# A hybrid attention and conv-FFN layer in float32: weight pieces of 1024 columns in place of 2048

## The chip, the core and the metric

The kernel runs on one core of a Trainium2 chip. The metric is the time of one execution on the device in microseconds (us), lower being better; a version's time is the median of several executions. PE is TensorE, DVE VectorE, ACT ScalarE, POOL GpSimd and SP SyncE, which issues most DMAs here.

## What is computed

One layer on 256 tokens of width 2048, in float32. A projection of x feeds three groups of dilated attention (8 heads of 128), a gated linear attention (4 heads) and two gates; their outputs are projected, gated, summed and projected again; a residual sum and layer norm follow, then a feed-forward net with a short convolution along the tokens, and a second residual sum and layer norm. Cut to the products with weights:

```
def _mixer(x, ...):
    parts = jnp.split(x @ w_in, cuts, axis=-1)      # q, k, v of 3 groups; gq gk gv gr g_low m_a m_b
    ...
    ya = ... @ w_proj_a
    yb = (o * jax.nn.silu(gr)) @ w_proj_b
    y = jax.nn.sigmoid(m_a) * ya + jax.nn.sigmoid(m_b) * yb
    return y @ w_out

def _conv_ffn(x, w_gate, w_up, conv_w, conv_b, w_down):
    g = x @ w_gate
    gc = conv_b + sum(conv_w[i] * shifted(g, i) for i in range(CONV_W))
    return (jax.nn.silu(gc) * (x @ w_up)) @ w_down

def reference(x, ...):
    x = _layernorm(ALPHA * x + _mixer(x, ...))
    return _layernorm(ALPHA * x + _conv_ffn(x, ...))
```

## The kernel before

**Products of split numbers.** Each float32 operand is split into a part that the matmul takes exactly (hi, ACT's copy in L136) and the rest (lo = value − hi, DVE's subtraction in L137). A product is hi·hi + hi·lo + lo·hi, so PE uses each piece of weights as hi and as lo.

**Pieces.** All weights arrive as a stream of pieces of 128 partitions × 2048 columns (1 MB), laid out on the host by `_stream` in the order of their use. `load` issues a piece's DMA on SP into a buffer: for the first layer's first part the tag raw (2 buffers), later the tag quarter (6 buffers; `home` says which). `two_parts` takes the tile for hi (tag whi, 3 buffers) and for lo (wlo, 2) and calls `split`. A buffer is free when its last reader is done, and a DMA or a split into it waits for that. So a load runs ahead of PE by as many buffers as there are.

**Three forms of product.** `b16` makes 128 columns of the output from one piece: 16 hi matmuls of 512 columns (L228), then 16 lo matmuls of 256 (L230). Its result is summed by `b_sum` (ACT pa in L252, DVE in L253), which frees the PSUM bank. `a_chunk` makes 256 × 512 outputs from two or four pieces (nf/4 pieces in the FFN's down projection), with hi, lo, hi matmuls for each 128 rows of weights (L260 to L262), and calls `pump` behind each piece, which writes the next side job (gate parts, transposes, residual sums) into the program at that place. `seven` makes a block product with seven products instead of eight; it sums pieces into each other first, on DVE (`add`, L339) or, for two of the sums, by an adding DMA on POOL's queue (`add_by_dma`, L342). In its `part`, the eight hi matmuls of a piece come ahead of its four lo ones (L326).

**Order.** Program text order isn't the order on the engines: a scheduler places each engine's instructions by modelled times and by the buffers in the pools, so that other pieces change what stands next to what. Within an engine the order is then fixed, and an instruction that waits holds all behind it.

**The stages**, by the profile's time: 0 to about 850 us the projections of x, with `gkq`, `qk` and the `seven` blocks side by side with attention; 850 to 1125 the projections ya (`yp`), `pb` and `wo`, with `gated_out` and its transposes (L808, fed by sg of L837 to L839) as a side job; at 1125 the residual sum r (L903), the statistics (L904, L888) and the first layer norm (L914, transposes L921); from 1150 the FFN. The FFN's first tiles come as three at once (`b16_three`); then each step f sums the gate (gbuf, L253), convolves (gr, L962 to L964), takes its silu (sg, L966), sums the up product (yb, L253), multiplies (yb, L974) and splits into h (L136, L137). While the FFN begins, `gain` scales the residual r by rows of layer norm parameters (L937, L938), which POOL fetches by DMA as tiles called row. The FFN runs in four parts, each followed by its down projection (`wd`). From 1873 us the last sums and the second layer norm run alone.

Of the kernel before, what the change touches and what calls it, by code (L numbers as in the profile page):

```python
# [35 lines left out]
FSPLIT = (16, 16, 8, 4)  # L36

# [20 lines left out]
def hybrid_layer(ctx: ExitStack, tc: tile.TileContext, wp, xt, wgl, gw, par, relb, onehot, rows, xk, out):  # L58
# [80 lines left out]
    home = ["raw", 2]  # L139

    def raw_tile(i, tag=None, bufs=None):
        tag, bufs = (tag, bufs) if tag else home
        return wpool.tile([P, 2048], F32, tag=tag, name=f"{tag}_{i}", bufs=bufs)
# [168 lines left out]
    def seven(name, xs, comb, i, store, by_dma=True):  # L312
# [41 lines left out]
        def p5():  # L354
            st["B12"] = [get(2), get(3)]
# [5 lines left out]
        def p6():  # L361
            st["B22"] = [get(4), get(5)]
# [26 lines left out]
        def p2():  # L389
            st["B21"] = [get(6), get(7)]  # L390
# [126 lines left out]
    def gkq(which, h):  # L517
        st = {}

        def f(j, before=(None,)):  # L520
            def g():
                ps = b16("gqk", xop, AT["gkq", which] + 2 * h + j, before)
# [8 lines left out]
    def head(h):  # L531
# [3 lines left out]
        def f(g, which):  # L535
            def t():
                ps = b16("qk", xop, AT["qk", h] + 2 * g + which)
# [187 lines left out]
    def gkq_tiles():  # L725
        for which in range(2):
            for h in range(GH):
                f = gkq(which, h)
                yield f(0, [pair_of_x(j) for j in range(4)] if not which and not h else (None,))
# [52 lines left out]
    for n in range(2):  # L782
        pss = a_chunk("m", xop, 16, AT["mb"] + 4 * n, 3)
# [5 lines left out]
    home[:] = "quarter", 6  # L789
# [73 lines left out]
    for n in range(4):  # L863
        g = [gate(1, n, t) for t in range(2)]
        pss = a_chunk("pb", by_pairs(OB), 16, AT["pb"] + 4 * n)
# [30 lines left out]
    for n in range(4):  # L896
# [3 lines left out]
        pss = a_chunk("wo", by_pairs(YT), 16, AT["wo"] + 4 * n)  # L900
# [45 lines left out]
    for part, nf in enumerate(FSPLIT):  # L946
# [5 lines left out]
        for f in range(f0, f0 + nf):  # L952
            if f == 0:
                first = AT["fgu"]
                three = dict(zip("gun", b16_three(("fg", "fu", "fg"), x1op, (first, first + 1, first + 2))))
            at = AT["fgu"] + 2 * f
# [10 lines left out]
            if f == 1:  # L967
                with tc.issue_after(held.ins):
                    ps = b16("fu", x1op, at + 1)
            else:  # L970
                ps = three["u"] if f == 0 else b16("fu", x1op, at + 1)
# [12 lines left out]
        for n in range(0, 4, 2):  # L984
            at = [AT["wd", part] + (n + i) * nf // 4 for i in range(2)]
# [36 lines left out]
def _stream():  # L1022
# [121 lines left out]
```

## Time and profile before

| | us |
|---|---|
| median of three executions | 1892.54 (1891.72 to 1896.99) |
| profiled execution | 1894.48 |
| its span on the core | 1892.8 |

| instructions in the profiled execution | count | mean |
|---|---|---|
| lo splits of whole pieces from quarter, DVE L137 | 312 | 2289 ns |
| hi splits of whole pieces from quarter, ACT L136 | 312 | 1917 ns |
| lo and hi splits of whole pieces from raw | 71 and 71 | 2288 and 1914 ns |
| sums of pieces, DVE L339 | 44 | 2284 ns |
| loads of 1 MB into quarter and into raw | 252 and 71 | 4.9 and 6.8 us to landing |
| adding DMAs, POOL L342, 1 MB | 36 | 12.4 us to landing |

The page of a profile gives each engine's busy time; a view by stretch gives the same for parts of the span, with the granted TensorE clock (PEclk, 1.00 is full speed) and what the 16 DMA engines moved. A view of waits says which engine waited for whom. In a timeline's row stand the start, the duration (of x instructions together), the engine, the line, the tiles (output <- inputs, with shapes), and in brackets the idle time ahead of it and what ended it.

### The profile page before, as it was taken

The page shows a single profiled execution, that of the slowest core. Times are in us where ns is not written, and L with a number is a line of the kernel's source. Part 1 is how long each engine was busy: PE and PEld are TensorE (multiplying, and loading weights), DVE is VectorE, ACT ScalarE, POOL GpSimd, SP SyncE. Part 2 cuts the span into 40 slices and gives each one's busy share as a digit, 9 for nine tenths or more (in the row PEclk, how much of TensorE's full clock was granted, in tenths as well). Part 3 has the DMA queues.
Part 4 walks back from the last instruction along what each step waited for, and adds up shares of the span by engine and source line. Part 5 has one row for each costly group of instructions (what it writes and reads, how often), then busy time and mean ns, then how long its engine had stood idle before and what let it go on. Part 6 is the DMA issues. An engine that isn't in the chain of part 4 may idle for free. (4 is left out here: it accounts for less than half of the span.)

```text
span 1892.8 us, 23057 instructions
## 1 busy us (share of the span) xinstructions
PE 1837.2 (97%) x9270; PEld 1548.0 (82%) x9270; DVE 1310.8 (69%) x1186; ACT 970.1 (51%) x963; POOL 121.9 (6%) x205
## 2 busy tenths in 40 slices
PE   7989999999999999999899998999999999999996
PEld 6778887888888888787788877888888888888885
DVE  6879978888797888764755557666546665456557
ACT  5457555555656565544643344454335554345442
POOL 0001000100101000001300001000000000000001
PEclk9999999999999999999999998999999999999998
DMA  8468986978979779794965546555555555565551
GB/s 304 157 251 275 318 307 207 326 234 263 329 230 327 231 274 331 214 325 163 333 224 195 202 160 217 179 195 183 200 189 189 189 190 193 187 243 182 196 178 45
DMA packets 80134, 432.21 MB, mean 228 GB/s; under 512 B 9857, under 2 KB 20124, under 8 KB 34076
## 3 DMA queue, kind: packets, MB, share of 16 engines
q1 hardware_dynamic: 50252, 345.06, 49.4%
q0 software_dynamic: 16240, 73.52, 15.5%
q10 hardware_dynamic: 13536, 12.16, 2.1%
q8 instruction: 72, 1.18, 0.2%
q14 instruction: 34, 0.28, 0.0%
HBM read 372.97 MB, written 21.14 MB: 208 GB/s over the span
## 5 line engine op out<-in xcount | busy, mean ns | idle before, releaser
L137 DVE TENSOR_TENSOR wlo<-quarter,whi 128x2048 fp32r<-128x2048 f32 x312 | 713.4, 2289 | 358.8 <-ACT whi L136 82.1
L136 ACT ACTIVATE whi<-quarter 128x2048 fp32r<-128x2048 f32 x312 | 597.4, 1917 | 479.1 <-PE wd_t L262 106.4
L137 DVE TENSOR_TENSOR wlo<-raw,whi 128x2048 fp32r<-128x2048 f32 (+1 forms) x75 | 165.2, 2203 | 47.3 <-ACT whi L136 23.7
L136 ACT ACTIVATE whi<-raw 128x2048 fp32r<-128x2048 f32 (+1 forms) x75 | 138.4, 1845 | 110.5 <-PE qk L228 43.2
L228 PE MATMUL qk<-x,whi 128*128 128x512 f32 x768 | 193.1, 399 | 1.5 <-ACT whi L136 1.5
L228 PE MATMUL fu<-x,whi 128*128 128x512 f32 x688 | 165.9, 394 | 5.5 <-DVE yb L253 5.5
L228 PEld LDWEIGHTS qk<-x,whi 128*128 128x128 f32 x768 | 142.0, 188 | 32.6 <-ACT whi L136 2.2
L228 PE MATMUL fg<-x,whi 128*128 128x512 f32 x672 | 160.2, 390 | 0.0
L228 PEld LDWEIGHTS fu<-x,whi 128*128 128x128 f32 x688 | 127.7, 190 | 30.6 <-issue 5.7
L228 PEld LDWEIGHTS fg<-x,whi 128*128 128x128 f32 x672 | 123.7, 188 | 24.0
L260 PE MATMUL wd_t<-whi,h 128*128 128x512 f32 x352 | 137.0, 389 | 0.0
L261 PE MATMUL wd_t<-wlo,h 128*128 128x512 f32 x352 | 137.0, 389 | 0.0
L262 PE MATMUL wd_t<-whi,h 128*128 128x512 f32 x352 | 136.9, 389 | 0.0
L230 PEld LDWEIGHTS qk<-x,wlo 128*128 128x128 f32 x768 | 98.4, 191 | 4.0 <-DVE wlo L137 0.3
L339 DVE TENSOR_TENSOR quarter<-quarter,quarter 128x2048 f32<-128x2048 f32 x44 | 100.3, 2284 | 0.4
L230 PE MATMUL qk<-x,wlo 128*128 128x256 f32 x768 | 99.7, 283 | 0.0
L230 PEld LDWEIGHTS fu<-x,wlo 128*128 128x128 f32 x688 | 88.2, 191 | 3.4
L230 PE MATMUL fu<-x,wlo 128*128 128x256 f32 x688 | 89.2, 283 | 0.0
L230 PEld LDWEIGHTS fg<-x,wlo 128*128 128x128 f32 x672 | 86.2, 191 | 3.3
L230 PE MATMUL fg<-x,wlo 128*128 128x256 f32 x672 | 87.2, 283 | 0.0
L260 PEld LDWEIGHTS wd_t<-whi,h 128*128 128x128 f32 x352 | 66.1, 188 | 13.7
L261 PEld LDWEIGHTS wd_t<-wlo,h 128*128 128x128 f32 x352 | 66.1, 188 | 13.6
(316 smaller groups left out, 2680.3 us busy)
## 6 DMA issues: line engine op xcount, KB each, us to landing
quarter<-in_wp SPq DMA_DIRECT2D x252, 1024.0 KB, 4.9
raw<-in_wp SPq DMA_DIRECT2D x71, 1024.0 KB, 6.8
quarter<-quarter POOLq DMA_DIRECT2D x36, 1024.0 KB, 12.4
row<-in_rows POOLq DMA_DIRECT2D x16, 256.0 KB, 4.6
sp<-c POOLq DMA_DIRECT2D x14, 256.0 KB, 10.9
bias<-bvd ACTq DMA_DIRECT2D x32, 96.0 KB, 4.6
v<-vs ACTq DMA_DIRECT2D x24, 128.0 KB, 2.9
m<-sp POOLq DMA_DIRECT2D x12, 256.0 KB, 4.9
```

The lines of the kernel that those rows point to most:

```text
L136: nc.scalar.activation(hi, src, AF.Copy)
L137: nc.vector.tensor_tensor(lo, src, hi.bitcast(F32), op=ALU.subtract)
L228: nc.tensor.matmul(ps, parts(kc)[0], opnd(kc), start=(kc == 0), stop=False)
L230: nc.tensor.matmul(ps[:, S:], parts(kc)[1], opnd(kc)[:, :S], start=False, stop=(kc == nk - 1))
L260: nc.tensor.matmul(ps, xh, hi, start=first, stop=False)
L261: nc.tensor.matmul(ps, xh, lo, start=False, stop=False)
L262: nc.tensor.matmul(ps, xl, hi, start=False, stop=last)
L339: tt(a, a, b, op=ALU.add)
```

## The change

A piece has 1024 columns instead of 2048 (512 KB), and each tag has twice as many buffers of half the size: raw 4, quarter 12, whi 6, wlo 4. The bytes are the same. The stream is cut in halves in the same order of use. `b16` takes two pieces, of eight blocks of 128 each; `a_chunk` takes one for each two blocks of 128 rows instead of four, and still calls `pump` where it did, behind every second piece. In `seven` the order hi, hi, lo is kept within a piece, so that there are four hi matmuls and then two lo ones. So 323 loads by SP become 646, 383 splits of whole pieces on ACT and as many on DVE become 766 each (the first piece, which was already cut in four slices of 512, stays in four), 44 sums on DVE become 88, and 36 adding DMAs become 72. PE has the same matmuls.

```
 FSPLIT = (16, 16, 8, 4)
+PC = 1024
...
-    home = ["raw", 2]
+    home = ["raw", 4]
...
         tag, bufs = (tag, bufs) if tag else home
-        return wpool.tile([P, 2048], F32, tag=tag, name=f"{tag}_{i}", bufs=bufs)
+        return wpool.tile([P, PC], F32, tag=tag, name=f"{tag}_{i}", bufs=bufs)
...
         n_blk[0] += 1
-        hi = wpool.tile([P, 2048], F32R, tag="quarter" if spare else "whi", name=f"whi_{n_blk[0]}", bufs=6 if spare else 3)
-        lo = wpool.tile([P, 2048], F32R, tag="quarter" if spare else "wlo", name=f"wlo_{n_blk[0]}", bufs=6 if spare else 2)
+        hi = wpool.tile([P, PC], F32R, tag="quarter" if spare else "whi", name=f"whi_{n_blk[0]}", bufs=12 if spare else 6)
+        lo = wpool.tile([P, PC], F32R, tag="quarter" if spare else "wlo", name=f"wlo_{n_blk[0]}", bufs=12 if spare else 4)
...
         n_blk[0] += 1
-        hi = wpool.tile([P, 2048], F32R, tag="whi", name=f"whi_{n_blk[0]}")
-        lo = wpool.tile([P, 2048], F32R, tag="wlo", name=f"wlo_{n_blk[0]}", bufs=2)
-        n = 2048 // len(before)
+        hi = wpool.tile([P, PC], F32R, tag="whi", name=f"whi_{n_blk[0]}", bufs=6)
+        lo = wpool.tile([P, PC], F32R, tag="wlo", name=f"wlo_{n_blk[0]}", bufs=4)
+        n = PC // len(before)
         for k, f in enumerate(before):
-            if f is not None:
-                f()
+            f()
...
-    by_cols = lambda ws: lambda kc: [a[:, kc * P : (kc + 1) * P] for a in ws]
-
-    def b16(name, opnd, i, before=(None,)):
-        return b_tile(name, by_cols(piece(i, before)), opnd, 16)
+    def by_cols(pcs):
+
+        return lambda kc: [a[:, (kc % 8) * P : (kc % 8 + 1) * P] for a in pcs[kc // 8]]
+
+    def b16(name, opnd, i, before=(None, None)):
+        n = len(before) // 2
+        pcs = [piece(i + k, before[k * n : (k + 1) * n]) for k in range(2)]
+        return b_tile(name, by_cols(pcs), opnd, 16)
...
-        ws = [by_cols(two_parts(load(i), spare=(i == idx[-1]))) for i in idx]
+        ws = [by_cols([two_parts(load(i + k), spare=(i == idx[-1])) for k in range(2)]) for i in idx]
...
         pss = [cbank(f"{name}_t{t}") for t in range(2)]
-        for k0 in range(0, nk, 4):
-            hi, lo = piece(i + k0 // 4)
-            for k in range(4):
+        for k0 in range(0, nk, 2):
+            hi, lo = piece(i + k0 // 2)
+            for k in range(2):
                 kc = k0 + k
...
                     a_part(pss[t], opnd(kc), hi[:, w], lo[:, w], t, kc == 0, kc == nk - 1)
-            pump(n_pump)
+            if k0 % 4:
+                pump(n_pump)
         return pss
...
-        pcs = [piece(i) for i in idx]
+        pcs = [[piece(i + k) for k in range(2)] for i in idx]
         pss = [[cbank(f"{name}_t{t}") for t in range(2)] for _ in pcs]
         for t in range(2):
-            for (hi, lo), ps in zip(pcs, pss):
+            for pair, ps in zip(pcs, pss):
                 for k in range(4):
-                    w = slice(k * 512, (k + 1) * 512)
+                    hi, lo = pair[k // 2]
+                    w = slice((k % 2) * 512, (k % 2 + 1) * 512)
...
             for w, which in ((hi, 0), (hi, 1), (lo, 0)):
-                for k in range(4):
-                    kc = 4 * p + k
+                for k in range(2):
+                    kc = 2 * p + k
...
         def get(k):
-            return load(i + k, "quarter", 6)
+            return [load(i + 4 * k + p, "quarter", 12) for p in range(4)]
         def p1():
-            st["T"] = [get(0), get(1)]
+            st["T"] = get(0)
             st["A"] = cbank(name + "A")
...
         def p5():
-            st["B12"] = [get(2), get(3)]
+            st["B12"] = get(1)
             for a, b in zip(st["T"], st["B12"]):
...
         def p6():
-            st["B22"] = [get(4), get(5)]
+            st["B22"] = get(2)
...
         g = [gate(0, n, t) for t in range(2)]
-        pss = a_chunk("yp", yop, 8, AT["pa"] + 2 * n)
+        pss = a_chunk("yp", yop, 8, AT["pa"] + 4 * n)
...
                 first = AT["fgu"]
-                three = dict(zip("gun", b16_three(("fg", "fu", "fg"), x1op, (first, first + 1, first + 2))))
-            at = AT["fgu"] + 2 * f
+                three = dict(zip("gun", b16_three(("fg", "fu", "fg"), x1op, (first, first + 2, first + 4))))
+            at = AT["fgu"] + 4 * f
...
         for n in range(0, 4, 2):
-            at = [AT["wd", part] + (n + i) * nf // 4 for i in range(2)]
+            at = [AT["wd", part] + (n + i) * nf // 2 for i in range(2)]
...
     def b(w, c, rows=2048):
-        out.append((w, 0, rows, c, P))
+        for k in range(0, rows, 1024):
+            out.append((w, k, 1024, c, P))
     def a(w, c, first, rows):
-        for k in range(first, first + rows, 512):
-            out.append((w, k, 512, c, 512))
+        for k in range(first, first + rows, 256):
+            out.append((w, k, 256, c, 512))
```

Left out are the same index arithmetic for `gkq`, the qk tiles, `m`, `pb`, `wo` and `fu`, and the same lists in `p2`.

Lines of the changed kernel stand up to six further down (L137 is L138, L253 is L257, L808 is L814, L903 is L909).

The scheduler then places instructions anew. Three places of the order on an engine follow, each before and with the change. The names carry the program's own running numbers, which differ between the two.

**DVE at the first layer norm**, where the residual r of the last columns is summed (the rows at L903, L909), and its statistics are taken (L904, L910). Before:

```order
L137 TENSOR_TENSOR wlo_1018_8571<-quarter_192_8568,whi_1018_8570 128x2048
L903 SCALAR_TENSOR_TENSOR r_983_8327<-r_983_8327,wo_t0_985_8331 128x512
L137 TENSOR_TENSOR wlo_1019_8577<-quarter_193_8574,whi_1019_8576 128x2048
L904 BN_STATS st0_7935<-r_983_8327 128x6
L903 SCALAR_TENSOR_TENSOR r_984_8329<-r_984_8329,wo_t1_986_8332 128x512
L888 BN_AGGR mv_991_8457<-st0_7935 128x2
```

with the change:

```order
L138 TENSOR_TENSOR wlo_1272_10052<-quarter_386_10049,whi_1272_10051 128x1024
L909 SCALAR_TENSOR_TENSOR r_1231_9772<-r_1231_9772,wo_t0_1233_9776 128x512
L138 TENSOR_TENSOR wlo_1273_10058<-quarter_387_10055,whi_1273_10057 128x1024
L910 BN_STATS st0_9308<-r_1231_9772 128x6
L909 SCALAR_TENSOR_TENSOR r_1232_9774<-r_1232_9774,wo_t1_1234_9777 128x512
L894 BN_AGGR mv_1243_9926<-st0_9308 128x2
```

A lo split (wlo) stands between the first r and its statistics in both; it has 2048 columns before and 1024 now.

**PE at the first transposes of `gated_out`** (pt, from sg) among the matmuls of yp, before:

```order
L260 MATMUL yp_t0_881_7072<-whi_883_7076,ya_801_6545 128x512
L261 MATMUL yp_t0_881_7072<-wlo_883_7077,ya_801_6545 128x512
L262 MATMUL yp_t0_881_7072<-whi_883_7076,ya_801_6545 128x512
L260 MATMUL yp_t1_882_7073<-whi_883_7076,ya_801_6545 128x512
L261 MATMUL yp_t1_882_7073<-wlo_883_7077,ya_801_6545 128x512
L262 MATMUL yp_t1_882_7073<-whi_883_7076,ya_801_6545 128x512
L260 MATMUL yp_t0_881_7072<-whi_883_7076,ya_801_6545 128x512
L261 MATMUL yp_t0_881_7072<-wlo_883_7077,ya_801_6545 128x512
L262 MATMUL yp_t0_881_7072<-whi_883_7076,ya_801_6545 128x512
L260 MATMUL yp_t1_882_7073<-whi_883_7076,ya_801_6545 128x512
L808 MATMUL pt_867_6981<-ident_87,sg_862_6968 128x128
L808 MATMUL pt_868_6990<-ident_87,sg_862_6968 128x128
```

with the change:

```order
L265 MATMUL yp_t1_1070_8162<-wlo_1083_8255,ya_1006_7727 128x512
L266 MATMUL yp_t1_1070_8162<-whi_1083_8254,ya_1006_7727 128x512
L264 MATMUL yp_t0_1095_8313<-whi_1097_8317,ya_1005_7726 128x512
L814 MATMUL pt_1080_8216<-ident_87,sg_1075_8203 128x128
L814 MATMUL pt_1081_8225<-ident_87,sg_1075_8203 128x128
L265 MATMUL yp_t0_1095_8313<-wlo_1097_8318,ya_1005_7726 128x512
L266 MATMUL yp_t0_1095_8313<-whi_1097_8317,ya_1005_7726 128x512
L264 MATMUL yp_t1_1096_8314<-whi_1097_8317,ya_1005_7726 128x512
```

Ten matmuls of the next chunk (yp_t0_881, yp_t1_882) stood ahead of the transposes; now one of them does (yp_t0_1095).

**DVE at the start of the FFN**, from the product yb·sg of the first step (L974, L980) to the sum yb of the next one (L253, L257), with the rows of `gain` (r, row) between. Before:

```order
L974 TENSOR_TENSOR yb_1027_8694<-yb_1027_8694,sg_1026_8692 128x256
L137 TENSOR_TENSOR wlo_1042_8808<-quarter_197_8805,whi_1042_8807 128x2048
L137 TENSOR_TENSOR h_1029_8699<-yb_1027_8694,h_1029_8699 128x256
L253 TENSOR_TENSOR gbuf1_6922<-fg_1023_8588,pa_1030_8702 128x256
L937 TENSOR_TENSOR r_984_8329<-r_984_8329,row_1153_9836 128x512
L938 TENSOR_TENSOR r_984_8329<-r_984_8329,row_1154_9839 128x512
L137 TENSOR_TENSOR wlo_1046_8854<-quarter_198_8851,whi_1046_8853 128x2048
L963 SCALAR_TENSOR_TENSOR gr_1031_8705<-gbuf1_6922,prm_92,gr_1031_8705 128x256
L964 SCALAR_TENSOR_TENSOR gr_1031_8705<-gbuf1_6922,prm_92,gr_1031_8705 128x256
L253 TENSOR_TENSOR yb_1035_8750<-fu_1034_8717,pa_1036_8751 128x256
```

with the change:

```order
L980 TENSOR_TENSOR yb_1282_10181<-yb_1282_10181,sg_1281_10179 128x256
L257 TENSOR_TENSOR gbuf1_8151<-fg_1278_10075,pa_1285_10189 128x256
L943 TENSOR_TENSOR r_1220_9620<-r_1220_9620,row_1404_11236 128x512
L138 TENSOR_TENSOR wlo_1299_10307<-quarter_394_10304,whi_1299_10306 128x1024
L138 TENSOR_TENSOR h_1284_10186<-yb_1282_10181,h_1284_10186 128x256
L969 SCALAR_TENSOR_TENSOR gr_1286_10192<-gbuf1_8151,prm_92,gr_1286_10192 128x256
L138 TENSOR_TENSOR wlo_1300_10313<-quarter_395_10310,whi_1300_10312 128x1024
L970 SCALAR_TENSOR_TENSOR gr_1286_10192<-gbuf1_8151,prm_92,gr_1286_10192 128x256
L944 TENSOR_TENSOR r_1220_9620<-r_1220_9620,row_1405_11239 128x512
L943 TENSOR_TENSOR r_1231_9772<-r_1231_9772,row_1417_11348 128x512
L257 TENSOR_TENSOR yb_1291_10243<-fu_1290_10210,pa_1292_10244 128x256
```

Between the two there were two whole lo splits, and now there are two halves. The sum gbuf, which stood behind the first lo split and h, now stands ahead of both halves. Three rows of `gain` are there instead of two, and of an earlier r: these sums come later with respect to the FFN.

More of the change, by code (lines that the diff above doesn't have):

```diff
@@ L389, in p2 @@
         def p2():
-            st["B21"] = [get(6), get(7)]
+            st["B21"] = get(3)
             for a, b in zip(st["T"], st["B21"]):
@@ L518, in gkq, with f @@
         st = {}
-        def f(j, before=(None,)):
+        def f(j, before=(None, None)):
             def g():
-                ps = b16("gqk", xop, AT["gkq", which] + 2 * h + j, before)
+                ps = b16("gqk", xop, AT["gkq", which] + 2 * (2 * h + j), before)
                 if not j:
@@ L536, in t @@
             def t():
-                ps = b16("qk", xop, AT["qk", h] + 2 * g + which)
+                ps = b16("qk", xop, AT["qk", h] + 2 * (2 * g + which))
                 if not which:
@@ L728, in gkq_tiles @@
                 f = gkq(which, h)
-                yield f(0, [pair_of_x(j) for j in range(4)] if not which and not h else (None,))
+                yield f(0, [pair_of_x(j) for j in range(4)] if not which and not h else (None, None))
                 yield f(1)
@@ L782, in hybrid_layer @@
     for n in range(2):
-        pss = a_chunk("m", xop, 16, AT["mb"] + 4 * n, 3)
+        pss = a_chunk("m", xop, 16, AT["mb"] + 8 * n, 3)
         for t in range(2):
@@ L788, in hybrid_layer @@
     drain()
-    home[:] = "quarter", 6
+    home[:] = "quarter", 12
     early.close()
@@ L864, in hybrid_layer @@
         g = [gate(1, n, t) for t in range(2)]
-        pss = a_chunk("pb", by_pairs(OB), 16, AT["pb"] + 4 * n)
+        pss = a_chunk("pb", by_pairs(OB), 16, AT["pb"] + 8 * n)
         for t in range(2):
@@ L899, in hybrid_layer @@
             nc.gpsimd.dma_start(R[t][n], xk[t * P : (t + 1) * P, n * 512 : (n + 1) * 512])
-        pss = a_chunk("wo", by_pairs(YT), 16, AT["wo"] + 4 * n)
+        pss = a_chunk("wo", by_pairs(YT), 16, AT["wo"] + 8 * n)
         for t in range(2):
@@ L968, in hybrid_layer @@
                 with tc.issue_after(held.ins):
-                    ps = b16("fu", x1op, at + 1)
+                    ps = b16("fu", x1op, at + 2)
             else:
-                ps = three["u"] if f == 0 else b16("fu", x1op, at + 1)
+                ps = three["u"] if f == 0 else b16("fu", x1op, at + 2)
             u = tmp("yb")
```

## The prediction

> **What bounds the kernel now.** I read the page's busy shares first, then the busy time by stretch, and then TensorE's waits.
>
> ```profile
> span 1892.8 us, 23057 instructions
> PE 1837.2 (97%) x9270; PEld 1548.0 (82%) x9270; DVE 1310.8 (69%) x1186; ACT 970.1 (51%) x963; POOL 121.9 (6%) x205
> core 0: us, PE busy (x) PEld busy (x) DVE busy (x) ACT busy (x) POOL busy (x), PEclk, DMA share, GB/s
> 0.00:47.00 47.00, 37.30 (x179) 28.97 (x180) 30.43 (x47) 27.40 (x37) 2.72 (x11) 1.00 0.83 304
> 47.00:95.00 48.00, 45.34 (x220) 35.16 (x219) 42.30 (x36) 22.96 (x22) 2.92 (x7) 0.93 0.45 159
> 95.00:142.00 47.00, 40.83 (x187) 32.98 (x187) 36.00 (x24) 26.78 (x27) 3.24 (x6) 0.96 0.68 252
> 142.00:189.00 47.00, 46.02 (x232) 38.78 (x232) 45.07 (x31) 32.99 (x31) 6.85 (x10) 1.00 0.89 275
> 189.00:236.00 47.00, 47.00 (x239) 40.02 (x239) 42.64 (x32) 27.64 (x23) 3.97 (x6) 1.00 0.98 317
> 236.00:520.00 284.00, 281.64 (x1427) 237.43 (x1426) 226.46 (x173) 164.62 (x142) 25.04 (x36) 1.00 0.85 278
> 520.00:850.00 330.00, 328.42 (x1676) 276.31 (x1675) 260.48 (x208) 193.31 (x190) 29.91 (x45) 1.00 0.84 275
> 850.00:946.00 96.00, 88.31 (x402) 71.01 (x401) 59.48 (x72) 55.08 (x73) 24.70 (x49) 0.96 0.71 251
> 946.00:1135.00 189.00, 184.69 (x824) 151.03 (x822) 105.64 (x82) 75.81 (x57) 4.28 (x8) 1.00 0.56 196
> 1135.00:1182.00 47.00, 41.13 (x217) 34.35 (x216) 36.22 (x57) 22.91 (x30) 8.03 (x15) 0.86 0.67 218
> 1182.00:1872.00 690.00, 690.00 (x3659) 596.95 (x3658) 409.40 (x407) 317.95 (x332) 4.24 (x8) 1.00 0.52 185
> 1872.00:1892.80 20.80, 6.47 (x29) 5.03 (x27) 16.67 (x24) 2.63 (x6) 5.99 (x4) 0.74 0.28 101
> ```
>
> The reader is to see that PE is the bound, and where it is not. PE is idle for 1892.8 − 1837.2 = 55.6 us: 9.7 in 0–47, 2.7 in 47–95, 6.2 in 95–142, 1.0 in 142–189, 3.9 in 236–850, 7.7 in 850–946, 4.3 in 946–1135, 5.9 in 1135–1182 and 14.3 in the tail. Where the granted clock reads under 1.00 matmuls run longer as well. In 1182–1872, a third of the kernel, PE is busy for 690.00 of 690.00 us while DVE has 281 and ACT 372 us left. The change adds no matmul and takes none away, so there is nothing to win there; it can lose only if a split comes late. All gain must come out of PE's waits:
>
> ```profile
> PE pt L808 <- issue: 5.8, 1, 5.8
> PE fu L228 <- DVE yb L253: 5.5, 1, 5.5
> PE pt L921 <- ACT r L914: 3.8, 2, 2.0
> PE vA L326 <- ACT whi L136: 3.5, 1, 3.5
> PE gqk L230 <- DVE wlo L137: 2.3, 1, 2.3
> ```
>
> (Us in total, times, longest.) These five are 20.9 us, at five places. The tail is a chain of DVE sums and normalisation behind the last matmuls, which holds no weight piece: 0.
>
> **The price of halves on DVE and ACT.** The same elements are split in twice as many instructions, so what an instruction costs beyond its elements is paid once more for each of 383 splits of whole pieces (312 in the row below, 71 from raw), on ACT (hi) and on DVE (lo), and on DVE for each of 44 sums.
>
> ```profile
> L137 DVE TENSOR_TENSOR wlo<-quarter,whi 128x2048 fp32r<-128x2048 f32 x312 | 713.4, 2289 | 358.8 <-ACT whi L136 82.1 <-PE fg L230 59.7 <-PE fu L230 57.1
> L137 DVE TENSOR_TENSOR x<-xraw,x 128x512 fp32r<-128x512 f32 x8 | 5.5, 692 | 8.0 <-ACT x L136 8.0
> L339 DVE TENSOR_TENSOR quarter<-quarter,quarter 128x2048 f32<-128x2048 f32 x44 | 100.3, 2284 | 0.4
> 63.44 4.49 DVE L137 TENSOR_TENSOR wlo<-quarter,whi 128x2048 fp32r<-128x2048 f32 x2
> ```
>
> No row has 1024 columns, so I bound it. From 692 ns at 512 and 2289 at 2048 the slope is 1.040 ns a column and the constant 160 ns: 1224 ns at 1024, and 160 ns more for each piece that is halved. But two splits in a row take 4.49 us, so one starts 2.20 after the other: 0.09 of the constant lies beneath the neighbour, and the halves then start 1.13 apart, 0.07 more per piece. With 427 halved DVE instructions that is 30 to 68 us of DVE, beside 582 us idle; on ACT at the same 0.16 it is 61 us beside 923 idle. Over the whole kernel this is hidden. Where DVE is nearly full it is not sure to be:
>
> ```profile
> 142.00:236.00 94.00, 58.52 (x26) 1.00 0.94 296
> 142.00:236.00 94.00, 18.54 (x10) 1.00 0.94 296
> ```
>
> (DVE's lo splits and its L339 sums alone, in 142–236.) 36 instructions are halved there: +2.5 us at 0.07, +5.8 at 0.16, against 94 − 45.07 − 42.64 = 6.3 us idle. I take 0.07, as the splits stand in long rows without a gap there, and 0 for PE: cover is 6.3 us of DVE. With that cover gone the cost is what stands beyond it. Against it stands that PE may start on half a piece 1.1 us sooner. Bounds for 47–850: −10 to +11 (the rivals below).
>
> [...]
>
> **Start: −0.8.**
>
> ```profile
> 18.68 1.91 ACT L136 ACTIVATE whi<-raw 128x2048 fp32r<-128x2048 f32 x1 [1.82 <-DMA raw<-in_wp]
> 20.64 1.65 PE L228 MATMUL gqk<-x,whi 128*128 128x512 f32 x6 [0.63 <-ACT whi L136]
> ```
>
> PE waits 0.63 for the second piece's hi split, 1.91 long, which itself waited for its load. With halves the first half's split is about 0.96 long. That removes the wait, and part of the smaller ones near it: 0.8, bounds 0 and 2 (no more than the 1.91). The earlier idle time of 0–47 is x and its small loads: unchanged.
>
> **47–142: 0.** PE's waits for lo (2.3) and for hi of vA (3.5) lie here. In the new order the small gate projection's matmuls stand in the middle of a piece, and vA's hi waits for one half split instead of a whole one (−0.9 to −1), but four half sums now stand ahead of its lo half, at up to 1.13 each. I cannot tell which is larger: 0, from −10 to +5.
>
> **Transposes at 905: +1.2.**
>
> ```profile
> 908.70 0.63 ACT L837 ACTIVATE sg<-gr 128x512 f32<-128x512 f32 x1 [2.55 <-DMA gr<-sp]
> 1299.35 3.82 PE L228 MATMUL fu<-x,whi 128*128 128x512 f32 x16
> ```
>
> PE's 5.8 us at pt L808 wait for sg, whose gr comes by DMA; that fetch stands behind the last attention splits on ACT. Before, ten matmuls of the next chunk stand ahead of the transposes, now one. A matmul is (3.82 − 0.39)/15 = 0.229 us, so nine fewer bring PE to the wait 2.06 us earlier, and the nine are done after it instead: their time was hidden in the wait and is no longer. One half hi split instead of a whole one stands ahead of the fetch, so it comes up to 0.9 earlier. 2.06 − 0.9 = +1.2, bounds 0 and +2.5.
>
> **First layer norm: −1.1.**
>
> ```profile
> 1125.92 2.29 DVE L137 TENSOR_TENSOR wlo<-quarter,whi 128x2048 fp32r<-128x2048 f32 x1
> 1128.12 0.69 DVE L904 BATCH_NORM_STATS2 st<-r 128x6 f32<-128x512 f32 x1
> ```
>
> A lo split of 2.20 us stands between the residual sum and the statistics, and from the statistics the chain runs through rs and r to pt L921, where PE waits. Now one half stands there: 2.20 − 1.13 = 1.07. Bounds: 0 if two halves stand there, −2.2 if none.
>
> **Start of the FFN: −2.9.**
>
> ```profile
> 1165.87 0.42 DVE L974 TENSOR_TENSOR yb<-yb,sg 128x256 f32<-128x256 f32 x1
> 1166.20 2.29 DVE L137 TENSOR_TENSOR wlo<-quarter,whi 128x2048 fp32r<-128x2048 f32 x1
> 1169.93 0.69 DVE L938 TENSOR_TENSOR r<-r,row 128x512 f32<-128x512 f32 x1 [0.17 <-DMA row<-in_rows]
> 1170.54 2.28 DVE L137 TENSOR_TENSOR wlo<-quarter,whi 128x2048 fp32r<-128x2048 f32 x1
> 1174.49 0.42 DVE L253 TENSOR_TENSOR yb<-fu,pa 128x256 f32<-128x256 f32 x1 [0.75 <-ACT pa L252]
> 1175.07 5.64 PE L228 MATMUL fu<-x,whi 128*128 128x512 f32 x16 [5.50 <-DVE yb L253]
> ```
>
> PE waits 5.50 us for the sum yb, which frees the bank. Between yb·sg (next start at 1166.20) and that sum stand two whole lo splits before; in the new order two halves, with gbuf ahead of both. Nine steps follow 1166.20 there: gbuf, h and the two steps of gr at 0.33 (as from 1165.87 to 1166.20), three r sums at 0.61 (as from 1169.93 to 1170.54), and two halves at 1.13, in all 5.4; so yb stands at 1171.6, 2.9 earlier. The sixteen matmuls after the wait take 5.64, not 3.82; if the shorter wait spares that too, another 1.8. The bounds are −4.7 and +1: the added r sum of a later row stands ahead of yb, and if its row lands late it holds yb, as the row at 1169.93 was waited for.
>
> **Loads.** Twice as many loads of 512 KB, in the same bytes of buffers.
>
> ```profile
> quarter<-in_wp SPq DMA_DIRECT2D x252, 1024.0 KB, 4.9
> row<-in_rows POOLq DMA_DIRECT2D x16, 256.0 KB, 4.6
> ```
>
> A half lands between the 4.6 of a quarter of the size and 4.9, so it is barely sooner. One 1 MB load per 4.9 us would be 214 GB/s; 317 are moved in 189–236, so loads overlap, and the landing time isn't paid one after another: 0. The 36 adding transfers of POOL become 72, issued beside idle time (POOL is busy for 6%): 0.
>
> **Sum:** −0.8 + 0 + 1.2 − 1.1 − 2.9 = −3.6, on the profiled execution's 1894.48 (span and 1.7 around it): 1890.9. That execution stands 1.9 above the median of 1892.54, so I forecast **1889**; with the places' own bounds 1885 to 1893.
>
> **Rivals.**
> *DVE becomes the bound in 47–236 (slower).* Halves cost the full 0.16, PE asks for lo after four hi matmuls instead of eight in the seven products, and DVE there has no time left. For it: 45.07 of 47 busy, in a stretch where one wlo after another stands without a gap. Against it: 0.07 by the pair of 4.49, and 47.00 of 47 PE busy in 189–236. Price: 5.8 us in 142–236 and about as much in 47–142 (+11 in all), which decides once the added time passes the 6.3 us idle. Time: 1889 + 11 = 1900.
> *The front's waits melt (faster).* With half pieces hi and lo come in time: 3.5 + 2.3 gone and, with no long wait, the clock stays up: (1 − 0.93)·48 + (1 − 0.96)·47 = 5.2. That is −11, so 1878.
> *The change does not do what it says at the FFN's start:* the row's DMA, which lands by its own queue, takes the place of the split, and yb is as late as before. Then −0.7 is left: about 1892.
> *Loads of half the size cannot keep up:* if they queued one behind another at 4.6 us each, 114 GB/s would not feed 296 in 142–236; that stretch would last 94·296/114 = 244 us, 150 more. The overlap above speaks against it. [...]
>
> **How the numbers follow.** Forecast 0.42, DVE bound 0.17, front melts 0.24, row in its place 0.15, loads 0.02. A measurement of this kernel can tell about 0.3%, 5.7 us, from no change. Faster than 1886.9: most of the melting case and a quarter of the forecast's, 0.35. Slower than 1898.2: most of the DVE case and the loads, 0.17. Within: 0.48. The range takes in the melting case and the DVE case up to their prices: 1878 to 1900.
>
> **What would show it.** Right: 1024-column splits of about 1.22 us, 1.13 apart; the FFN wait at yb down to some 2.6 us; one half split between r and the statistics; transposes reached with a longer wait (about 7 us); PE busy for all of 1182–1872. Wrong: PE waits <- DVE wlo by the tens of us in 47–850, DVE full there; a wait of yb behind a row; a clock under 1.00 in new places; or waits of PE in the FFN.

## The result, and the profile after

The changed kernel takes 1881.24 us, a median of six executions (1878.05 to 1884.94), against 1892.86 us for the kernel before in the same series (1891.72 to 1896.99). The ratio is 0.9936 with an interval of 0.9919 to 0.9952: 0.64% faster, about 12 us. In a second series it was 0.9943 (0.9929 to 0.9957). 1889 us was forecast, with "within 0.3%" as the likeliest outcome. The time lies in the range of 1878 to 1900, near its lower end; it lies outside the 1885 to 1893 of the places' own bounds, and the gain is three times the 3.6 us of the sum.

Of the changed kernel's profiled execution (1883.29 us) the page's busy shares, and the view by stretch with the columns as before:

```profile
span 1881.6 us, 25449 instructions
PE 1835.3 (98%) x9270; PEld 1549.8 (82%) x9270; DVE 1348.2 (72%) x1613; ACT 1037.2 (55%) x1346; POOL 153.1 (8%) x241
0.00:47.00 47.00, 39.88 (x200) 31.70 (x201) 35.63 (x64) 32.43 (x51) 2.72 (x11) 1.00 0.86 313
47.00:95.00 48.00, 44.90 (x213) 35.18 (x212) 42.31 (x45) 20.81 (x26) 2.92 (x7) 0.93 0.49 170
95.00:142.00 47.00, 43.35 (x202) 35.91 (x201) 39.49 (x40) 33.80 (x43) 6.08 (x10) 0.93 0.80 282
142.00:189.00 47.00, 46.62 (x237) 39.56 (x236) 46.12 (x52) 33.58 (x42) 8.10 (x12) 1.00 0.89 254
189.00:236.00 47.00, 44.58 (x215) 36.23 (x214) 39.55 (x41) 26.65 (x32) 5.12 (x7) 1.00 0.92 302
236.00:520.00 284.00, 281.12 (x1418) 238.03 (x1417) 234.18 (x255) 177.79 (x213) 38.18 (x51) 0.99 0.88 279
520.00:850.00 330.00, 328.77 (x1679) 276.98 (x1678) 267.08 (x305) 208.62 (x272) 42.69 (x60) 1.00 0.87 276
850.00:946.00 96.00, 88.28 (x407) 72.28 (x406) 61.33 (x87) 57.77 (x91) 24.75 (x49) 0.96 0.74 252
946.00:1135.00 189.00, 185.33 (x823) 150.55 (x821) 110.53 (x120) 81.11 (x88) 4.28 (x8) 0.99 0.57 190
1135.00:1182.00 47.00, 47.00 (x271) 41.08 (x270) 41.18 (x69) 27.84 (x42) 8.03 (x15) 0.98 0.82 261
1182.00:1862.00 680.00, 680.00 (x3600) 588.07 (x3599) 414.91 (x523) 334.15 (x446) 4.23 (x8) 1.00 0.57 185
```

One row changed altogether: 1135 to 1182, the start of the FFN, where PE was idle for 5.87 us at a mean clock of 0.86 and is now busy throughout at 0.98. The front (0 to 142) lost idle time and 189 to 236 gained some. DVE is busy for 37 us more and ACT for 67, almost all of it beside PE's work; in the FFN proper PE still has no idle time.

PE's waits now, in us in total, times and longest; those at fu are gone:

```profile
PE pt L814 <- issue: 7.7, 1, 7.7
PE gqk L228 <- ACT whi L137: 6.5, 3, 3.3
PE ps L465 <- DVE s L467: 4.2, 3, 2.9
PE vD L332 <- DVE wlo L138: 3.1, 1, 3.1
PE pt L927 <- ACT r L920: 2.7, 2, 2.0
```

The price of a half, from the page's groups, one row of DVE's timeline, and the page's row of the loads (KB each, us to landing):

```profile
L138 DVE TENSOR_TENSOR wlo<-quarter,whi 128x1024 fp32r<-128x1024 f32 x624 | 747.6, 1221 | 354.2 <-PE wd_t L265 84.2
L137 ACT ACTIVATE whi<-quarter 128x1024 fp32r<-128x1024 f32 x624 | 655.8, 1057 | 478.6 <-PE wd_t L266 95.9
270.54 2.36 DVE L138 TENSOR_TENSOR wlo<-quarter,whi 128x1024 fp32r<-128x1024 f32 x2 [3.35 <-PE qk L230]
quarter<-in_wp SPq DMA_DIRECT2D x504, 512.0 KB, 4.5
```

A half takes 1221 ns (1224 was worked out), and two in a row start 2.36 − 1.22 = 1.14 apart (1.13). A half lands in 4.5 us, where a whole piece took 4.9 (4.6 to 4.9 was expected).

**Where the 11 us are.** Kernels of this study do the same products in nearly the same order, so the start of a tile's first or last matmul can be compared between profiles. The table gives its place relative to the profile before, in us (negative is earlier), from PE's timelines; the last column is what is won between the FFN's first matmul (fg, 1137.8 before) and its first down projection (wd_t, 1327.2 before), so at the FFN's start and in its first part. The e-numbers are the experiments below.

| kernel | last gqk (194.7) | last qk (839.0) | first yp_t (892.0) | last yp_t (947.8) | last keep (1128.8) | first fg (1137.8) | first wd_t (1327.2) | fg to wd_t |
|---|---|---|---|---|---|---|---|---|
| changed | −5.9 | −0.7 | −2.9 | −2.1 | −1.8 | −2.7 | −11.0 | −8.3 |
| changed, again (e11) | −3.5 | −0.5 | −2.7 | −0.6 | −0.3 | −1.2 | −9.5 | −8.3 |
| changed, rows late (e2) | −3.2 | −1.1 | −3.2 | −3.3 | −2.9 | −3.8 | −12.2 | −8.4 |
| rows late (e1) | 0.5 | 0.6 | 2.4 | 3.4 | 3.4 | 3.2 | 0.6 | −2.7 |
| late halves (e3) | −2.9 | −3.0 | −3.9 | −3.7 | −3.7 | −3.9 | −11.1 | −7.2 |
| early halves (e4) | −2.8 | 1.1 | −0.2 | −0.2 | −0.2 | −0.2 | −0.2 | 0.0 |
| transposes later (e5) | −4.4 | −3.2 | −5.2 | −4.9 | −4.8 | −5.0 | −11.8 | −6.8 |
| quarters (e8) | −1.4 | 19.8 | 17.9 | 18.0 | 18.0 | 16.2 | 9.3 | −6.9 |
| four pieces (e9) | 0.7 | 0.4 | 0.2 | 0.3 | 0.3 | 0.4 | −6.8 | −7.2 |
| two pieces (e10) | −2.6 | −2.7 | −2.8 | −2.9 | −2.9 | −2.9 | −5.7 | −2.8 |

Up to the first fg, e1, e9 and e10 have the instructions of the kernel before in the same order, and their first fg still stands at +3.2, +0.4 and −2.9. So a place in one profile says little below some 3 us; a difference between two places within a profile, away from the front, says more (from the last qk to the first yp_t these three still range from −0.2 to +1.8). The three profiles of the changed program agree on those: −8.3, −8.3 and −8.4 at the FFN's start, −2.2, −2.2 and −2.1 from the last qk to the first yp_t, −0.9 at the layer norm.

**The start of the FFN.** DVE's timeline of the changed kernel there:

```profile
1156.39 0.69 DVE L944 TENSOR_TENSOR r<-r,row 128x512 f32<-128x512 f32 x1
1156.99 0.69 DVE L943 TENSOR_TENSOR r<-r,row 128x512 f32<-128x512 f32 x1
1157.59 0.42 DVE L257 TENSOR_TENSOR yb<-fu,pa 128x256 f32<-128x256 f32 x1
1157.92 0.68 DVE L944 TENSOR_TENSOR r<-r,row 128x512 f32<-128x512 f32 x1
1158.52 0.42 DVE L980 TENSOR_TENSOR yb<-yb,sg 128x256 f32<-128x256 f32 x1
1158.86 0.42 DVE L257 TENSOR_TENSOR gbuf<-fg,pa 128x256 f32<-128x256 f32 x1
...
1164.40 0.41 DVE L257 TENSOR_TENSOR yb<-fu,pa 128x256 f32<-128x256 f32 x1
```

From yb·sg to the next yb: 1164.40 − 1158.52 = 5.9 us, against 1174.49 − 1165.87 = 8.6 before. That is the 2.7 us nearer (2.9 was forecast). But yb·sg itself also comes 7.35 us earlier, of which 2.7 are the earlier start of the FFN: another 4.6 us that the sum didn't have. No row sum waits for its DMA any more, and of the sixteen row sums six now come after yb·sg, where two did: four fewer stand ahead of it. Of the 8.3 us, 0.8 lie elsewhere, in the FFN's first three tiles: from the first fg to the first hi matmul of the next fu it is 19.6 us (1154.78 − 1135.14), and 20.4 before (1158.27 − 1137.84).

### The profile page after: what moved, and what is told of

It is laid out like the page before. It is cut to its first block, busy times and chain, and to the rows that moved or that the text cites. A ratio compares the mean times of both kernels' runs of the same rounds, so it can differ in the third digit from the quotient of the medians.

```text
span 1881.6 us, 25449 instructions
## 1 busy us (share of the span) xinstructions
PE 1835.3 (98%) x9270; PEld 1549.8 (82%) x9270; DVE 1348.2 (72%) x1613; ACT 1037.2 (55%) x1346; POOL 153.1 (8%) x241
## 4 chain that ended last, share of the span: by engine, by line
PE 86%; DMA 4%; DVE 2%; issue 1%; ACT 1%; DVEq 0%; SPq 0%; ACTq 0%; POOLq 0%
PE qk L228 9%; PE fu L228 8%; PE fg L228 8%; PE fu L230 4%; PE qk L230 4%; PE fg L230 4%; PE wd_t L264 4%; PE wd_t L266 4%; PE wd_t L265 4%; DMA quarter<-in_wp 2%; PE pb_t L266 2%; PE pb_t L265 2%; PE pb_t L264 2%; PE wo_t L264 2%; PE wo_t L265 2%; PE wo_t L266 1%
## 5 line engine op out<-in xcount | busy, mean ns | idle before, releaser
L138 DVE TENSOR_TENSOR wlo<-quarter,whi 128x1024 fp32r<-128x1024 f32 x624 | 747.6, 1221 | 354.2 <-PE wd_t L265 84.2
L137 ACT ACTIVATE whi<-quarter 128x1024 fp32r<-128x1024 f32 x624 | 655.8, 1057 | 478.6 <-PE wd_t L266 95.9
L137 ACT ACTIVATE whi<-raw 128x1024 fp32r<-128x1024 f32 (+1 forms) x146 | 151.4, 1044 | 86.4 <-PE qk L228 38.1
L138 DVE TENSOR_TENSOR wlo<-raw,whi 128x1024 fp32r<-128x1024 f32 (+1 forms) x146 | 173.3, 1205 | 30.6 <-ACT whi L137 10.8
L345 DVE TENSOR_TENSOR quarter<-quarter,quarter 128x1024 f32<-128x1024 f32 x88 | 104.4, 1217 | 0.4
L348 POOL DMA_DIRECT2D quarter<-quarter x72 | 62.9, 873 | 321.7 <-DMA quarter<-in_wp 175.0
```

The lines of the kernel that those rows point to most:

```text
L137: nc.scalar.activation(hi, src, AF.Copy)
L138: nc.vector.tensor_tensor(lo, src, hi.bitcast(F32), op=ALU.subtract)
L345: tt(a, a, b, op=ALU.add)
L348: nc.gpsimd.dma_start(a, b, accum_op=ALU.add)
```

## The experiments

Each ratio is against runs of the kernel before on the same chip. Line numbers move by a few with each edit.

**e1 and e2: the row sums out of the way.** Theory A: the gain is made on DVE's queue at the FFN's start. Theory B: finer pieces are needed. In e1 on the kernel before, in e2 on the changed one:

```
-            nc.vector.tensor_tensor(a, a, row(2, n), op=ALU.mult)
-            nc.vector.tensor_tensor(a, a, row(3, n), op=ALU.add)
+            with tc.issue_after(summed_up[-1].ins):
+                nc.vector.tensor_tensor(a, a, row(2, n), op=ALU.mult)
+                nc.vector.tensor_tensor(a, a, row(3, n), op=ALU.add)
...
-            nc.vector.tensor_tensor(u, u, sg, op=ALU.mult)
+            summed_up.append(nc.vector.tensor_tensor(u, u, sg, op=ALU.mult))
```

> The kernel before with whole pieces; only the sixteen row sums of gain are held on DVE behind the product yb*sg of an FFN step five or later. Theory A (the gain of the change comes from DVE's queue at the start of the FFN, where row sums and whole splits stand ahead of the sum yb that frees PE's bank): PE's 5.5 us wait at fu goes to under 1 us, and the half clock behind it with it; FFN reached 6 to 8 us earlier, time about 1885 to 1887 us. Theory B (only finer pieces can do that, since two whole lo splits of 2.2 us still stand ahead of yb): 2 us or more of the wait stay, time 1889 to 1891. Everything ahead of the FFN within 0.5 us of before under both.

Measured: 1891.12 us, ratio 0.9986 (0.9977 to 0.9996). Theory A failed in this form. With no row sum near, DVE's and PE's timelines of e1 read:

```profile
1173.07 2.29 DVE L137 TENSOR_TENSOR wlo<-quarter,whi 128x2048 fp32r<-128x2048 f32 x1 [0.86 <-PE fg L230]
1175.28 0.42 DVE L253 TENSOR_TENSOR yb<-fu,pa 128x256 f32<-128x256 f32 x1
1175.84 5.44 PE L228 MATMUL fu<-x,whi 128*128 128x512 f32 x16 [2.81 <-DVE yb L253]
```

The sum yb stands behind a whole lo split, which waits for PE to be done with the piece that holds its buffer. So PE waits 2.81 us for a split that PE itself held up: half of the wait is left, and −2.7 stands in the table. That e1 is 3.2 us late at the first fg, with the instructions of before up to there, was in neither theory.

> The changed kernel with the same hold on the row sums. Theory A: nothing is left to remove at the FFN's start, so 0, within 2 us of the changed kernel (1879 to 1884 us). Theory B: the same. A wait that the row sums hide elsewhere would show as more than 3 us.

Measured: 1881.42 us, 0.9932 (0.9918 to 0.9946), the changed kernel's time: nothing was left there.

**e3 and e4: halves late, halves early.** The kernel before with its loads, buffers and sums; only splits come in halves, in e3 from wo to the FFN's step 3, in e4 ahead of wo:

```
-        split(hi, lo, raw)
+        m = 2 if halve[0] else 1
+        for k in range(m):
+            c = slice(k * 2048 // m, (k + 1) * 2048 // m)
+            split(hi[:, c], lo[:, c], raw[:, c])
```

> The kernel before (1 MB loads, buffers of 2048 columns), with splits in halves only from the output projection wo through the FFN's step 3. Theory A: the wait at the FFN's start falls from 5.5 to under 1.5 us and the layer norm's chain is 1 us shorter: 1883 to 1887 us. Theory B (the gain is spread, by finer pieces everywhere): 1889 to 1892, the wait keeping 3 us or more.

> The kernel before (1 MB loads, buffers of 2048 columns), with splits in halves only ahead of wo, so in 0 to 1038 us. Theory A: the front's waits change places but sum to about the same, within 4 us of before (1889 to 1897 us), with the 5.5 us wait at the FFN's start still there. Theory B: 6 us or more faster (under 1887). A third theory, DVE's added instructions cost PE time: 1897 or more.

Measured: e3 1884.89 us, 0.9959 (0.9943 to 0.9974), with no wait at fu; e4 1892.91 us, 0.9998 (0.9988 to 1.0008), with the wait at fu (5.7) in place. Halves ahead of 1038 us neither gain nor cost, halves from there to the FFN's step 3 gain two thirds of the whole. The 1 us at the layer norm that was expected of e3 did not come: there a half stands ahead of each of the two last statistics, and PE's wait behind them is 3.7 us, as before (3.8).

**e5: the largest wait left.** On the changed kernel:

```
+    side.extend([lambda: None] * 2)
     side.extend(gated_out(h) for h in range(GH))
...
-        nc.tensor.matmul(ps, xl, hi, start=False, stop=last)
+        latest[:] = [nc.tensor.matmul(ps, xl, hi, start=False, stop=last)]
...
-            OB.extend(transposed("ob", h, g, P_NG))
+            with tc.issue_after(latest[0].ins):
+                OB.extend(transposed("ob", h, g, P_NG))
...
-                three = dict(zip("gun", b16_three(...)))
+                with tc.issue_after(summed.ins):
+                    three = dict(zip("gun", b16_three(...)))
```

> The changed kernel with two edits: the side jobs gated_out start two pumps later and their transposes on PE are held behind the 24th matmul of yp's second chunk, and the lo splits of the FFN's first three pieces are held on DVE behind the last statistics of the first layer norm. Theory A (PE's wait at the first transposes is a fixed landing time of gr, that matmuls can stand in for): 23 more matmuls stand ahead, 23 x 0.229 = 5.3 us, so the 7.7 us wait falls to about 2.4 or less, and the layer norm's chain is one half split (1.1 us) shorter: 6 us faster than the changed kernel, about 1875 us. Rival (the fetch is asked for later too, or the next chunk pb then waits for the last transposes): the wait stays over 5 us or comes back at pb, 1879 to 1883.

Measured: 1882.48 us, 0.9936 (0.9922 to 0.9949): nothing won. PE's waits of e5:

```profile
PE pt L816 <- issue: 3.2, 1, 3.2
PE pt L816 <- DVE sg L847: 3.1, 1, 3.1
```

The first wait lost 4.5 us, and 3.1 came back at the next transposes, which wait for the second half of sg. The rival was right in the time, and that the wait comes back, though not at pb: the 23 matmuls hide the first fetch and not the second. The second edit won nothing either. Held behind the statistics, five half splits now stand on DVE ahead of x1f, which the last transposes wait for. From the last keep to the first fg e5 gains 0.2 us where the changed kernel gains 0.9, and at the FFN's start 6.8 in place of 8.3. With two edits in one run, the worth of each isn't shown apart.

**e6 and e7: loads in halves, without and with splits in halves.** The kernel before with its buffers and sums whole:

```
-        nc.sync.dma_start(raw, wp[i])
+        for k in range(2):
+            c = slice(k * 1024, (k + 1) * 1024)
+            nc.sync.dma_start(raw[:, c], wp[i, :, c])
```

In e7 each split is also made in two halves of 1024 columns, as in e3 but everywhere.

> The kernel before with each 1 MB load in two DMAs of 512 KB; buffers, splits and sums stay whole. Theory A (the gain is in the splits at the FFN's start): 1890 to 1895 us, the 5.5 us wait at fu still there. Rival (finer loads bring the gain): 1887 or less. Third (DMAs of half the size cost bandwidth): over 1897, with waits of ACT for loads in 142 to 520.

Measured: 1898.87 us, 1.0021 (1.0012 to 1.003): 4 us slower, which is the time of the third theory. Its sign came in part: in 142 to 520 ACT's hi splits wait 16 us for loads, against 9 before. Its profile (span 1895.1, the low end of its executions) has PE waiting for hi splits of gqk:

```profile
PE gqk L230 <- ACT whi L136: 10.1, 3, 5.0
```

The longest of these, 5.0, is that of the first matmul, where the kernel before waits 4.3 for x; so this row is not the 4 us. The same two waits of PE as before stand at the transposes (5.7) and at fu (4.8). That halved loads bring no gain by themselves is shown; what makes them cost 4 us is not.

> The kernel before with loads and splits in halves, but buffers of 2048 columns, which come free as a whole, and whole sums. Theory A: all that the change gains needs no smaller buffers: 1880 to 1885 us, no wait at fu at the FFN's start. Rival (buffers that come free by halves carry part of it): 1885 to 1890.

Measured: 1885.65 us, 0.9952 (0.9938 to 0.9966). By the letter that is the rival's range, by 0.65 us. But the interval overlaps that of the changed kernel (0.9919 to 0.9952), so it decides nothing between the two theories; no profile of it is used here.

**e8: one step on, quarters.** The changed kernel with `PC = 512`, each tag with twice as many buffers again, and all loops and indices to match.

> The changed kernel taken one step on: pieces of 512 columns (256 KB), four times the buffers of a quarter of the size. DVE gets 854 more instructions at 0.07 to 0.16 us, 60 to 137 us in all, 10 to 22 of them in 47 to 236, where 21 us are idle; ACT up to 157 us more. Theory A (finer pieces cost DVE time that shows where DVE is nearly full, and nothing is left to gain at the FFN's start): 1883 to 1900 us, with more waits of PE for DVE in 47 to 300. Rival (the finer the better): 1878 or less.

Measured: 1900.38 us, 1.0037 (1.0024 to 1.005), 0.4 us above the range of theory A. The split's group of DVE, its busy time in 520 to 850 by stretch, and two of PE's waits:

```profile
L138 DVE TENSOR_TENSOR wlo<-quarter,whi 128x512 fp32r<-128x512 f32 x1248 | 806.2, 687 | 322.9 <-PE wd_t L265 88.0 <-PE qk L230 46.9 <-PE fu L230 40.7
520.00:850.00 330.00, 319.52 (x1618) 268.03 (x1617) 278.60 (x499) 222.24 (x426) 72.30 (x93) 0.99 0.91 270
PE vA L332 <- DVE wlo L138: 6.4, 4, 3.4
PE po L501 <- ACT o L722: 3.7, 1, 3.7
```

By 839 us it is 19.8 us behind, with PE idle for 10.5 us in 520 to 850 where it was idle for 1.2 with halves; at the FFN's start it gains 6.9, not far from the halves' 8.3. So the price of small pieces is real, and halves cost nothing that the times show. Where it is paid is not worked out in full: PE's waits for lo splits grow from 4.6 us with halves to 12.4, and those for ACT's result o at po from 0.9 to 3.7. Loads of 256 KB are an unlikely cause: ACT's hi splits wait 20 us for them in all, and 57 for the halves.

**e9 and e10: the place itself.** The kernel before with four, or two, of its 383 splits of whole pieces in halves:

```
-            return two_parts(load(i))
+            return two_parts(load(i), parts=2 if 3 <= i - AT["fgu"] <= 6 else 1)      # e10: 5 <=
```

> The kernel before, with only four of its 383 splits of whole pieces in halves: the fourth to seventh piece of the FFN (fu of step 1, fg and fu of step 2, fg of step 3), whose lo splits stand on DVE around the first sums. Theory A (the change's gain is made at that place): no wait at fu, 6 to 8 us faster than before, 1885 to 1888 us. Rival (halves of all pieces are needed, since the row sums or the pieces ahead hold DVE too): less than 3 us.

> The same with only the sixth and seventh piece in halves, the two whose lo splits stand between yb*sg and the sum yb; the two ahead of them stay whole. Theory A as the prediction had it (only the stretch from yb*sg to yb gets shorter): the 5.5 us wait loses 2.5 to 3 us and no more, 3 to 4 us faster than before. Rival (these two are enough): no wait left, 6 to 8 us.

Measured: e9 1887.45 us, 0.9963 (0.995 to 0.9976); e10 1890.19 us, 0.9985 (0.9976 to 0.9994). Of e10 the ends of the stretch on DVE and PE's wait, and then of e9 the same two sums and PE's matmuls of that step:

```profile
1162.71 0.42 DVE L976 TENSOR_TENSOR yb<-yb,sg 128x256 f32<-128x256 f32 x1
1169.23 0.42 DVE L255 TENSOR_TENSOR yb<-fu,pa 128x256 f32<-128x256 f32 x1
1169.79 5.23 PE L230 MATMUL fu<-x,whi 128*128 128x512 f32 x16 [3.05 <-DVE yb L255]
```

```profile
1163.13 0.41 DVE L976 TENSOR_TENSOR yb<-yb,sg 128x256 f32<-128x256 f32 x1
1168.15 0.42 DVE L255 TENSOR_TENSOR yb<-fu,pa 128x256 f32<-128x256 f32 x1
1170.08 3.82 PE L230 MATMUL fu<-x,whi 128*128 128x512 f32 x16
```

With the two pieces between yb·sg and yb in halves, the stretch is 6.5 us instead of 8.6, PE's wait 3.05 instead of 5.50, and 2.8 us are won: what the prediction worked out, and no more. With the two pieces ahead of them in halves as well (e9), yb·sg too comes 3.1 us earlier (measured against each profile's first fg: 1163.13 − 0.4 against 1165.87), no wait is left, and the sixteen matmuls there take 3.82 us and not 5.23. In the kernel before, sixteen take 3.82 too where the granted clock is 1.00 (at 1299.35), and 5.64 behind its wait, with the clock at 0.50 from 1172 to 1178. Four splits of 383 make 7.2 of the 8.3 us.

Only 0.8 us of that step are shorter splits as such, ahead of the first gbuf. From gbuf to yb·sg e9 takes 6.4 us and e10 8.5, though three half splits stand there in e9 and one whole split in e10. What went are four of six row sums and 1.0 us of waits for a row's DMA: with other pieces, the scheduler placed these sums later. e1 shows that their place alone doesn't do it. Row sums out of the way with whole splits win 2.7 us (e1), two halved splits with the row sums in place win 2.8 (e10), and both together win 7.2 (e9), since then the wait is gone and the slow matmuls behind it with it.

**e11: the changed kernel once more.** No edit.

> The changed kernel once more, for a second profile: what is the program's and what the execution's. Theory A: the FFN's first products are done 8 us nearer to the layer norm than before, again; the place up to 840 us differs between the two profiles by up to 4 us, as it does between profiles of kernels that have the same instructions there. Rival (the front's gain by 195 us and its loss by 440 us belong to the change): both come again.

Measured: 1883.70 us, 0.9943 (0.9929 to 0.9957). In the table the 8.3 us come again. The front's lead by 195 us comes again too, and so does its loss by 839 us. The rival was right about the loss: 2.1 to 5.2 us from the last gqk to the last qk in the three profiles, where kernels with the instructions of before there (e1, e3, e9, e10) have 0.3 or less. The lead is less sure: −3.2 to −5.9 against −2.9 to +0.7. Their sum is 1.1 us or less in all three.

## Why the prediction came out as it did

**Bound and price: right.** PE bounds the kernel, the FFN has no idle PE before (690.00 of 690.00 us busy) or after (680.00 of 680.00), and DVE's 427 more instructions cost 37.4 us of busy time (1348.2 − 1310.8, 0.088 each), between the 0.07 and 0.16 of the bounds, hidden as forecast. At the whole constant of 160 ns, an estimate from the rows of 692 ns for 512 columns and 2289 for 2048, it would be 68; the duration of one half, 1221 ns, agrees with that constant (1224), and the busy time doesn't, since neighbours overlap (1.14 us from start to start).

**Start −0.8 and 47–850 at 0: right in sum, in part by luck.** PE's idle time in 0–47 fell by 2.6, more than the bound of 2, but a first matmul that is 1 us earlier is also seen in e9, which has the instructions of before. Of the two waits in 47–142 that the prediction names, that for lo (2.3) and vA's for hi (3.5) went, and one of vD for lo (3.1) and one of gqk for hi (2.6) came. By the last qk at 839 us the changed program is 0.5 to 1.1 us ahead, after a lead of 3 to 6 us that no term had and that was lost again. Halved splits alone, in e4, made no measurable difference in the whole stretch.

**Transposes +1.2: right within its bounds.** From the first to the last yp_t the three profiles lose 0.8, lose 2.1 and gain 0.1, 0.9 in the mean, which spreads more than the term. PE's wait grew from 5.8 to 7.7 (9.1 in e11, 6.9 in e2), as forecast.

**Layer norm −1.1: right.** −0.9 in all three. The half stands there as the order had it:

```profile
1124.14 1.22 DVE L138 TENSOR_TENSOR wlo<-quarter,whi 128x1024 fp32r<-128x1024 f32 x1
1125.27 0.69 DVE L910 BATCH_NORM_STATS2 st<-r 128x6 f32<-128x512 f32 x1
```

**850–892: not in the sum.** The changed program gains 2.2 us between the last qk and the first yp_t. Before, PE was idle for 7.7 us in 850–946, of which the prediction treated the 5.8 at the transposes alone. The rest is mostly a wait for s, the sum of the attention scores on DVE, and s stands behind a whole lo split; two rows of the kernel before, and then the same place with the change:

```profile
853.50 2.29 DVE L137 TENSOR_TENSOR wlo<-raw,whi 128x2048 fp32r<-128x2048 f32 x1 [4.64 <-ACT whi L136]
856.05 0.70 PE L459 MATMUL ps<-qk 128*128 128x256 f32 x2 [1.61 <-DVE s L461]
```

```profile
850.97 1.23 DVE L138 TENSOR_TENSOR wlo<-raw,whi 128x1024 fp32r<-128x1024 f32 x1 [1.49 <-PE m_t L265]
852.56 0.60 PE L465 MATMUL ps<-qk 128*128 128x256 f32 x2
```

The wait is 0.8 to 1.9 us in e1, e3, e9 and e10 too, whose splits are whole there, 0.7 with halved splits in whole buffers (e4), and gone in all three profiles of the changed program. So this is the mechanism of the FFN's start at another place, read from the traces; no run changes this place alone.

**Start of the FFN −2.9: the mechanism was right and the term too small; it measured −8.3.** The step that failed is "Nine steps follow 1166.20 there". The nine steps were right: 2.7 us by the profile after; in e10, where they alone are shorter, 2.8 were won. But 1166.20 was kept as a fixed starting point, and the same edit shortens what stands ahead of it: the first gbuf and yb·sg also wait behind lo splits and row sums, so yb·sg moved 4.6 us on its own. Halving the two pieces ahead as well, which e9 does and e10 doesn't, is worth 4.4 us (7.2 − 2.8), much of it by the row sums that come later with it. The prediction saw one more row sum behind yb·sg, and did not count the four fewer ahead of it. With the wait gone altogether, the slow matmuls behind it went too (sixteen in 5.64 us before, in 3.82 now), which the prediction had only as a bound (−4.7 was its most).

**The rivals.** DVE as the bound did not come: 46.12 of 47 us busy in 142–189 with PE at 46.62. Even one size further down (e8) DVE isn't full, with 51 us idle in 520–850, though PE waits for it more. The melting front named the right size, 11 us, at the wrong place: the front's lead is given back by 839 us. That the time lies in the stated range is luck to this extent: the lower end of 1878 was this rival's price, and the forecast's own bounds end at 1885. A row in place of the split didn't come: no row was waited for. Loads of half the size kept up: 302 GB/s in 189–236 (317 before) and 282 in 95–142 (252 before). A price of smaller loads shows at most in e6's 0.21%, whose cause is open, and in a part of e8's 0.37%.

The sum by measured terms, each a mean of the three profiles, is −0.8 − 2.1 + 0.9 + 0.3 − 0.9 − 8.3 = −10.9, against 11.6 us between the medians; the 0.3 lie between the last yp_t and the last keep.

## What to carry to other kernels

Where an in-order engine carries bulk splits and also the small sums that free the matmul engine's banks, the length of one bulk instruction is what a small sum waits for (here 2.29 us of a whole lo split, 1.22 of a half); at the few places where that chain sets the end, cutting a handful of pieces is worth nearly as much as cutting all (7.2 of 8.3 us from four of 383, together with the small sums that the scheduler placed anew). To price such an edit, follow the chain back to where the engine last had slack, and move its starting point too: a stretch worked out from a fixed start gives a part of the gain. And look for the size at which the pieces begin to cost: halves were free here, quarters cost 20 us in the first 840.

## What was not expected of the hardware

Two profiles of one instruction order differ by up to 6 us by the FFN's start (first fg at +3.2 in e1 and −2.9 in e10), about half of it from the first 195 us (last gqk at +0.5 and −2.6); medians of several executions are needed for anything less. A load of half the size is barely sooner there, 4.5 us against 4.9. And loading by halves into whole buffers was 0.21% slower (e6), while the same halves into buffers of their own went with the fastest kernel.
